# The chunked scan of an RWKV-7 layer: an even pace for its triangular solve, block-wise transfers, the group norm's weight and bias on GpSimd, key copies ahead of masks

## The chip, the cores and the metric

The kernel runs on one core of a Trainium2 chip. The metric is the device time of one execution in microseconds, the median over several. The core has TensorE (PE), VectorE (DVE), ScalarE (ACT), GpSimd (POOL) and SyncE (SP), whose queue issues most of the DMAs. Each engine takes its instructions in order and waits on semaphores that others set.

## The reference

A trunk of two layers with 1024 channels runs over two requests that share the weights: a prompt of 256 tokens and a sample of 1024. Layer 0 mixes tokens with a bidirectional RWKV-7 scan, layer 1 with neighbourhood attention, and each is followed by a squared-ReLU MLP. The change touches the scan and the group norm behind it. Cut to those, with 16 heads of 64 channels:

```
def step(S, inp):                       # in both directions, d = 0 and 1
    r_t, w_t, k_t, v_t, a_t, b_t = inp
    sa = einsum('bhvk,bhk->bhv', S, a_t)
    S = S * w_t + sa[..., None] * b_t + v_t[..., None] * k_t
    return S, einsum('bhvk,bhk->bhv', S, r_t)
y = scan forward + scan backward
mu, var = mean and variance of y over the 64 channels of a head
y = ((y - mu) * rsqrt(var + GN_EPS)) * lnx_g + lnx_b
y = y + bonus * v                       # bonus: one number per head and token
out = (y * g) @ w_o
```

## The kernel before

**Jobs and steps.** The scan works on chunks of 64 tokens. A job is sixteen chunks of a pair of heads (one head in each half of the 128 partitions): jobs 0 and 1 take four head pairs of the prompt each, four chunks long, and jobs 2 to 9 one head pair each of the sample. That is 10 jobs of 16 steps; in each step the forward direction does one chunk and the backward direction another. Within a step (`scan_step`) PE adds products of keys and values into the PSUM banks `bx` and `by`, ACT copies a part out as `up` (L1031), PE multiplies it by the chunk's inverse `Q`, ACT copies the result as `u` (L1051), PE adds its products, and ACT scales the next state `S` (L1066). The output goes to `y`: by an ACT copy in the first eight steps (L1072), by a DVE addition in the last eight (L1074). Each step also prepares the keys of a later step: PE makes `kps` (L952, a PSUM tile with one buffer), DVE multiplies it by a mask into `zz` (L957), and ACT copies the rest as `ll` (L962).

**The inverse.** Each chunk and direction needs the inverse of a triangular 64x64 matrix. In `scan_job`, for each of eight pieces of a job (direction d and group g of four chunks), a load `eab` (L813), products `aps` on PE (L821), a mask on DVE into `za` (L824) and a store to the DRAM scratch `dd` (L827) prepare it. `mload` (L842) loads the 32x32 diagonal blocks back, with one block in each partition, the second direction's as `mraw`, which GpSimd copies transposed into `mt` (`mtr`, L851, four copies). Then DVE solves all blocks at once: 31 steps, one rank-1 update each, a multiplication `tmp` (L867) and an addition to `q` (L869); the first and last steps are one instruction (L863). The result goes through DRAM (`qd`, L880 and L883) into the halves of the tiles `qq` and `qx` (L901, L902), and two products on PE with ACT copies in between (`yps`/`yt`, `qps`/`qq`, L913 to L930) merge the diagonal blocks to the full inverse.

**The norm.** `scan_post` follows each half of a job's output, at clocks 12.9 and 16.9 of the job, so that its last part lies in steps 1 and 5 of the next: bonus times v on DVE into `bv` (L1104), mean, centred `y` (L1112), squares on ACT into `ysq` (L1116), variance (L1120), a reciprocal root and the scaling of `y` (L1137). PE transposes `y` into `zps` and `bv` into `vps` (L1143). ACT scales `zps` by the norm's weight and adds the bias, which stand per partition after the transposition (L1149, four instructions), DVE adds `vps` (L1153), and eight DMAs store the tile `zt` into `z_d` (L1158).

**Order.** All this is written as closures with times, `at(t, f)`, in units of a step; a job's clock starts at 16 times its number. The list is sorted by time and emitted, and PE, DVE, ACT and GpSimd take the instructions in just that order; SP's queue is ordered by the framework. Items of job 0 with times up to `hi` run beside the projections before the scan. PSUM tiles with the tag `aps` (`aps`, `yps`, `qps`, `zps`, `vps`) share two buffers.

Of the kernel before, what the change touches and what calls it, by code (L numbers as in the profile page):

```python
# [29 lines left out]
V_QG, V_KG, V_LG, V_LB = 136, 137, 138, 154  # L30
NVEC = 170
# [18 lines left out]
class Trunk:  # L50
# [50 lines left out]
    def l0_proj(self):  # L101
# [361 lines left out]
        def begin():  # L463
            bctx.close()
            self.scan_begin()

            hi, c = -5.0, ((-41.0, tb), (-18.0, tb + 6.0), (-5.0, tb + 17.0))
            for x in self.todo:
                if x[3] < 3 and x[0] <= hi:
                    (x0, t0), (x1, t1) = c[:2] if x[0] < -18.0 else c[1:]  # L470
# [247 lines left out]
    def scan_begin(self):  # L718
# [9 lines left out]
                                        (("vv", [P, 16, 64]), ("qq", [P, 16, 2, 64]), ("qx", [P, 16, 2, 64])))  # L728
# [21 lines left out]
    def scan(self):  # L750
# [7 lines left out]
        grow(self.r_x, "qx", [P, 16, 2, 64])  # L758
        for r in (self.r_q, self.r_x):
            nc.gpsimd.memset(r[0][1], 0.0)  # L760
        grow(self.r_za, "za", [P, 4, 64], 12)
        self.r_x4 = [[], 0]
# [24 lines left out]
    def scan_job(self, j):  # L787
# [14 lines left out]
        T0 = -36.0  # L802

        def first():
            J["dd"] = [self.dsc.tile([16, 2, 64, 64], F32, name="dd", tag="dd") for _ in range(2)]
        at(T0 - 2.0, first, E)
        for n, (d, g) in enumerate(order):
# [18 lines left out]
            def store(d=d, g=g):  # L826
                nc.sync.dma_start(J["dd"][d].rearrange("c e s t -> (e s) c t")[:, 4 * g:4 * g + 4, :], J["za", d, g])  # L827
# [8 lines left out]
        def mload():  # L836
            mt = self.er.tile([P, 32, 32], F32, name="mt", tag="mt")
            raw = self.er.tile([P, 32, 32], F32, name="mraw", tag="mraw")
            for d in range(2):
                for b in range(2):  # L840
                    o, bs = 64 * d + 32 * b, slice(32 * b, 32 * b + 32)
                    nc.sync.dma_start((mt, raw)[d][o:o + 32], J["dd"][d].rearrange("c e s t -> (c e) s t")[:, bs, bs])  # L842
# [12 lines left out]
        T3, load = T2, 0.0  # L855
        for jj in range(31, 0, -1):
# [15 lines left out]
            if load > 930.0:  # L872
                T3, load = T3 + 0.5, 0.0
# [17 lines left out]
        at(T3 - 6.0, qclear)  # L891

        def qld():
            src = lambda x, o: J["qd"][x, o:o + 32].rearrange("(c e) s t -> e s c t", e=2)
            for d in range(2):
                for b in (d, 1 - d):
                    o, bs = 64 * d + 32 * b, slice(32 * b, 32 * b + 32)
                    for e in range(2):
                        q0 = slice(64 * e + 32 * b, 64 * e + 32 * b + 32)
                        if b == d:  # L900
                            nc.sync.dma_start(J["qx"][q0, :, d, bs], src(1 - d, o)[e])  # L901
                        nc.sync.dma_start(J["Q"][q0, :, d, bs], src(d, o)[e])  # L902
        at(T3 + 1.6, qld)

        for n, (d, g) in enumerate(order):
            m, c0 = grp[g]

            def merge1(c, d=d, g=g):
                if c == 0:
                    J["yps", d, g] = w4(self.pa.tile([P, 512], F32, name="yps", tag="aps"))  # L910
                for c in (c, c + 1):
                    for es, eo in HALVES:
                        mm(J["yps", d, g][es, c], J["za", d, g][es, c], J["qx"][es, 4 * g + c, d], start=True, stop=True)  # L913
# [13 lines left out]
            def merge2c(d=d, g=g):  # L927
                for e in range(2):
                    rl = slice(64 * e + 32 * d, 64 * e + 32 * d + 32)
                    nc.scalar.copy(J["Q"][rl, 4 * g:4 * g + 4, d, 32 - 32 * d:64 - 32 * d], J["qps", d, g][rl, :, :32])  # L930

            t = 2 * n - 5 if n > 1 else -3 + n
            for dt, f in ((0.12, lambda f=merge1: f(0)), (0.14, lambda f=merge1: f(2)), (0.5, merge1c), (0.76, lambda f=merge2: f(0)), (0.78, lambda f=merge2: f(2)), (0.97, merge2c)):
                at(t + dt, f)
# [7 lines left out]
        for q in range(16):  # L942
# [24 lines left out]
        def vload():  # L967
            J["v"] = self.nxt(self.r_v)
            vd = self.scr["v_d"]
            parts = [(grp[0][0], grp[0][1], 0, 16)] if grp[0][1] else [(m, c0, 4 * g, 4) for g, (m, c0) in enumerate(grp)]  # L970
            for m, c0, k, n in parts:
                rows = slice(c0 * L, (c0 + n) * L)
                for e, (es, eo) in enumerate(HALVES):
                    nc.sync.dma_start(J["v"][eo, k:k + n], vd[rows, m * P + 64 * e:m * P + 64 * e + 64].rearrange("(c s) v -> s c v", s=L))
        at(-5.423, vload)
# [110 lines left out]
    def scan_post(self, at, J, grp, left):  # L1086

        nc = self.nc
        for half in range(2):
# [15 lines left out]

            def p1(st=st, y=y):
# [32 lines left out]
            def tr(src, nm, st=st):  # L1139
                ps = st[nm] = self.pa.tile([P, 4, 2, 64], F32, name=nm, tag="aps")  # L1140
                swap = self.ident.rearrange("p (e t) -> p e t", e=2)[:, ::-1]
                for b in range(4):
                    nc.tensor.matmul(ps[:, b], src()[:, b // 2, b % 2 * 2:b % 2 * 2 + 2], swap, start=True, stop=True)  # L1143

            def trc(st=st, runs=runs):
                zt = st["zt"] = self.yp.tile([P, 4, 2, 64], F32, name="zt", tag="zt", bufs=1)
                for x, (m, c0) in enumerate(runs):
                    for e in range(2):
                        nc.scalar.activation(zt[:, 2 * x:2 * x + 2, e], st["zps"][:, 2 * x:2 * x + 2, e], AF.Identity, scale=self.v(V_LG, 2 * m + e), bias=self.v(V_LB, 2 * m + e))  # L1149
# [10 lines left out]
            if left == 0 and half == 1:  # L1160
                when = (-2.0, -0.1, 0.0, 0.1, 0.2, 0.3, 0.4, 0.5, 0.6, 0.7, 0.8, 0.9, 1.0)
            else:
                when = (0.2, 0.6, 0.95, 1.15, 1.45, 1.6, 1.75, 1.95, 2.3, 3.36, 4.36, 3.52, 4.6)
            bv = lambda st=st: st["bv"].rearrange("p (x c) v -> p x c v", x=2)
            for dt, f in zip(when, (p0, p1, p2, p2b, p2c, lambda f=p3: f(0), lambda f=p3: f(1), lambda f=p3: f(2), p4,
                                    lambda f=tr, y=y: f(y, "zps"), lambda f=tr, bv=bv: f(bv, "vps"), trc, p5)):
# [714 lines left out]
def host_layout(inputs):  # L1881
# [25 lines left out]
        np.tile(i["na_q_g"][0], 2)[:, None], np.tile(i["na_k_g"][0], 2)[:, None],  # L1907
        *(np.tile(i[nm].reshape(16, 64).T, (2, 1)) for nm in ("rw_lnx_g", "rw_lnx_b"))], 1)
# [36 lines left out]
```

## Time and profile before

| | us |
|---|---|
| median of 3 runs | 4202.09 (4198.46 to 4203.69) |
| the profiled execution, its own time | 4200.77 |
| its span, first to last instruction | 4199.0 |
| first and last `up` copy of the scan, from the span's start | 761.9 and 1444.4 |
| PE busy over the span | 3811.6 (91%) |
| DVE, ACT, GpSimd busy over the span | 2490.4, 1549.7, 1141.8 |

A row of a timeline reads: start, duration, engine, line, operation, output and inputs; in brackets the engine's idle time just before it and what ended it. A row of the waits reads: the waiting engine, tile and line, the one that released it, and then the time in total, the number of waits and the longest. A row of groups has the count, busy time and the mean of one in ns, and behind the bar the idle time before. A row of windows has the length of the stretch, the busy time of PE, of PE's weight loads, of DVE, ACT and GpSimd with their instruction counts, TensorE's granted clock, the busy share of the DMA engines and GB/s. The scan, 682.5 of the span's 4199.0 us by its first and last `up`, is the part to look at.

### The profile page before, as it was taken

To read this page: it belongs to the slowest core of one execution; us is meant where nothing else is said; L and a number is where in the kernel's file an instruction comes from. 1 tells how busy PE (TensorE), PEld (TensorE's weight loads), DVE (VectorE), ACT (ScalarE), POOL (GpSimd) and SP (SyncE) were. 2 spreads that over 40 slices of the span, in tenths; PEclk is the share of its full clock that TensorE was granted. 3 is DMA by queue.
4 is the path that set the end of the run, shared out by engine and by line. 5 is a ranking of instruction groups with operands and counts; after the bars stand their busy time and mean duration, and the time that the engine had idled before them with its cause. 6 is when DMAs were issued, how large, how long until landed. Compare 5 with 4: busy or idle time off the path is not lost.

```text
span 4199.0 us, 88054 instructions
## 1 busy us (share of the span) xinstructions
PE 3811.6 (91%) x35700; PEld 3197.4 (76%) x35700; DVE 2490.4 (59%) x4870; ACT 1549.7 (37%) x3711; POOL 1141.8 (27%) x1014
## 2 busy tenths in 40 slices
PE   7887879677777799999999999999989999999999
PEld 4664669666766688888888889776767788888888
DVE  7888973556666357555555561456565755555555
ACT  6776651344444442111111132455554211111111
POOL 5440001001010134222222250334344422222222
PEclk8996889899999899999999999999999999999999
DMA  3326565756564351111111115333333111111111
GB/s 110 88 95 205 197 192 148 181 147 164 144 166 119 87 166 46 41 41 41 38 37 38 41 56 165 90 80 74 81 101 128 61 41 36 36 41 41 36 36 61
DMA packets 443255, 387.81 MB, mean 92 GB/s; under 512 B 223296, under 2 KB 367904, under 8 KB 442848
## 3 DMA queue, kind: packets, MB, share of 16 engines
q1 hardware_dynamic: 394336, 314.92, 26.7%
q10 hardware_dynamic: 46704, 61.35, 4.3%
q8 instruction: 280, 4.59, 0.5%
q0 software_dynamic: 1808, 5.90, 0.4%
q14 instruction: 127, 1.04, 0.1%
HBM read 272.05 MB, written 121.24 MB: 94 GB/s over the span
## 4 chain that ended last, share of the span: by engine, by line
PE 58%; DVE 4%; ACT 3%; DMA 2%; issue 1%; POOL 1%; SPq 1%; ACTq 0%; DVEq 0%; POOLq 0%
PE ps L96 17%; PE ps L98 17%; PE ps L97 17%; PE pt L1802 1%; PE op L1860 1%; PE by L989 1%; PE nst L1597 1%; PE s L1784 1%; PE s L1787 1%; PE vps L512 1%; PE vps L513 1%; PE vps L514 1%; PE bx L989 1%; PE kps L952 0%; DMA vs_d<-v_d 0%
## 5 line engine op out<-in xcount | busy, mean ns | idle before, releaser
L1417 DVE TENSOR_TENSOR x<-ps,x 128x256 f32<-128x256 f32 x1488 | 814.7, 597 | 629.0 <-PE ps L98 628.6
L96 PE MATMUL ps<-ah,whi 128*128 128x512 f32 (+1 forms) x2304 | 843.5, 366 | 4.2 <-ACT whi L90 3.5
L98 PE MATMUL ps<-ah,wlo 128*128 128x512 f32 (+1 forms) x2304 | 824.3, 358 | 2.0 <-POOL wlo L91 2.0
L97 PE MATMUL ps<-al,whi 128*128 128x512 f32 (+1 forms) x2304 | 823.8, 358 | 0.0
L91 POOL TENSOR_TENSOR wlo<-raw,whi 128x1024 fp32r<-128x1024 f32 (+1 forms) x178 | 390.2, 2192 | 861.1 <-ACT whi L90 833.1
L96 PE MATMUL ps<-hh,whi 128*128 128x512 f32 (+1 forms) x1536 | 547.3, 356 | 13.0 <-DVE x L1417 13.0
L98 PE MATMUL ps<-hh,wlo 128*128 128x512 f32 (+1 forms) x1536 | 546.1, 356 | 0.0
L97 PE MATMUL ps<-hl,whi 128*128 128x512 f32 (+1 forms) x1536 | 545.6, 355 | 0.0
L96 PEld LDWEIGHTS ps<-ah,whi 128*128 128x128 f32 x2304 | 438.7, 190 | 78.7 <-issue 13.1
L98 PEld LDWEIGHTS ps<-ah,wlo 128*128 128x128 f32 x2304 | 437.6, 190 | 68.1 <-POOL wlo L91 2.9
L97 PEld LDWEIGHTS ps<-al,whi 128*128 128x128 f32 x2304 | 438.5, 190 | 60.2 <-issue 1.1
L90 ACT CAST whi<-raw 128x1024 fp32r<-128x1024 f32 (+1 forms) x206 | 200.8, 975 | 703.0 <-PE ps L97 627.9
L96 PEld LDWEIGHTS ps<-hh,whi 128*128 128x128 f32 x1536 | 291.8, 190 | 56.6 <-DVE x L1417 15.8
L98 PEld LDWEIGHTS ps<-hh,wlo 128*128 128x128 f32 x1536 | 291.7, 190 | 41.1
L97 PEld LDWEIGHTS ps<-hl,whi 128*128 128x128 f32 x1536 | 291.7, 190 | 41.1
L1396 POOL TENSOR_TENSOR rl<-rl 128x512 f32<-128x512 f32 (+1 forms) x192 | 174.1, 907 | 500.5 <-PE ps L98 458.3
L1395 ACT ACTIVATE rl<-ps 128x512 f32<-128x512 f32 (+1 forms) x192 | 100.8, 525 | 546.3 <-PE ps L98 546.3
L1398 ACT CAST hh<-rl 128x512 fp32r<-128x512 f32 (+1 forms) x192 | 105.5, 549 | 320.9 <-POOL rl L1396 320.9
L1399 DVE TENSOR_TENSOR hl<-rl,hh 128x512 fp32r<-128x512 f32 (+1 forms) x192 | 119.4, 622 | 151.5 <-ACT hh L1398 151.0
L989 PE MATMUL by<-up,qq 64*64 64x64 f32 x1280 | 75.6, 239 | 111.1 <-ACT up L1031 106.7
L1795 POOL TENSOR_TENSOR s<-s,mx 128x384 f32<-128x384 f32 (+1 forms) x154 | 116.9, 769 | 213.8 <-DVE mx L1794 144.9
L957 DVE TENSOR_TENSOR zz<-kps,cst 128x512 f32<-128x512 f32 x160 | 110.2, 688 | 79.9 <-PE kps L952 79.9
(308 smaller groups left out, 7685.9 us busy)
## 6 DMA issues: line engine op xcount, KB each, us to landing
x<-x_d SPq DMA_DIRECT2D x88, 512.0 KB, 4.6
raw<-in_w_down_dram SPq DMA_DIRECT2D x64, 512.0 KB, 3.2
raw<-in_w_up_dram SPq DMA_DIRECT2D x64, 512.0 KB, 3.1
eab<-x_d SPq DMA_DIRECT2D x80, 256.0 KB, 6.0
x_d<-ar ACTq DMA_DIRECT2D x32, 512.0 KB, 2.8
x_d<-bk ACTq DMA_DIRECT2D x32, 512.0 KB
bs<-tab SPq DMA_DIRECT2D x128, 96.0 KB, 3.8
v_d<-vt ACTq DMA_DIRECT2D x80, 128.0 KB, 4.3
```

Source lines behind the costliest of these rows:

```text
L90: nc.scalar.copy(hi[:, cs], raw)
L91: lo_eng.tensor_tensor(out=lo[:, cs], in0=raw, in1=hi[:, cs].bitcast(F32), op=ALU.subtract)
L96: mm(ps, sh, mh, start=first, stop=False)
L97: mm(ps, sh, ml, start=False, stop=False)
L98: mm(ps, sl, mh, start=False, stop=last)
L957: nc.vector.tensor_tensor(out=z, in0=src[:, :, :, :P], in1=self.mask[d].unsqueeze(1).unsqueeze(1).to_broadcast([P, 2, 2, P]), op=ALU.mult)
L989: mm = lambda out, a, b, start, stop: nc.tensor.matmul(out, a, b, start=start, stop=stop, skip_group_check=True)
L1396: nc.gpsimd.tensor_tensor(out=r[:, :n], in0=r[:, :n], in1=r[:, :n], op=ALU.mult)
L1398: nc.scalar.copy(hh[:, :n], r[:, :n])
L1399: nc.vector.tensor_tensor(out=hl[:, :n], in0=r[:, :n], in1=hh[:, :n].bitcast(F32), op=ALU.subtract)
L1417: nc.vector.tensor_tensor(out=xv, in0=ps[:, :n], in1=xv, op=ALU.add)
L1795: nc.gpsimd.tensor_tensor(out=s[:, :nk], in0=s[:, :nk], in1=mx[:, 2:3].to_broadcast([P, nk]), op=ALU.mult)
```

## The change

It has five parts.

- **The solve's pace.** The 31 rank-1 updates come 0.8 of a slot apart instead of 0.5 (a slot holds two of them), from step 9 of the job two ahead to step 5 of the job just ahead; before, they lay between step 14.5 and step 6. The preparation of each job (`T0`) starts earlier.
- **Whole blocks.** `dd` holds the diagonal blocks only, each contiguous, so that `mload` reads rows of 4 KB; a piece's store is four DMAs instead of one. `qx` has half its width, the loads of `qx` and `qq` come one pair at a time instead of in a burst, the merge's first product is 32 columns wide, its copies `yt` go into tiles that hold the constant part already, and its last copy is one instruction instead of two, half a step later.
- **The norm.** Weight and bias come as a tile `lnx`, with the values along the free axis. GpSimd adds the bias to `bv` and multiplies `y` by the weight. PE transposes both into the same PSUM tile, and one ACT copy makes `zt`. That tile now has the tag `ysq`, so it shares the one buffer of the squares.
- **Key copies.** `ll` is emitted ahead of `zz`.
- **Products.** The products `aps` stand between the step's last matmuls and the key products in odd steps, and v is loaded in two parts.

```diff
-            hi, c = -5.0, ((-41.0, tb), (-18.0, tb + 6.0), (-5.0, tb + 17.0))
+            hi, c = -6.0, ((-42.0, tb), (-19.0, tb + 6.0), (-6.0, tb + 17.0))
...
+        self.r_yt = [[[], 0], [[], 0]]
...
-        T0 = -36.0
+        T0 = (-37.0, -37.0, -39.0)[j] if j < 3 else -41.5
...
-            J["dd"] = [self.dsc.tile([16, 2, 64, 64], F32, name="dd", tag="dd") for _ in range(2)]
+            J["dd"] = [self.dsc.tile([2, 16, 2, 32, 32], F32, name="dd", tag="dd") for _ in range(2)]
...
             def store(d=d, g=g):
-                nc.sync.dma_start(J["dd"][d].rearrange("c e s t -> (e s) c t")[:, 4 * g:4 * g + 4, :], J["za", d, g])
+                for e in range(2):
+                    for b in range(2):
+                        o, bs = 64 * e + 32 * b, slice(32 * b, 32 * b + 32)
+                        nc.sync.dma_start(J["dd"][d][b, 4 * g:4 * g + 4, e].rearrange("c s t -> s c t"), J["za", d, g][o:o + 32, :, bs])
...
-            for d in range(2):
-                for b in range(2):
-                    o, bs = 64 * d + 32 * b, slice(32 * b, 32 * b + 32)
-                    nc.sync.dma_start((mt, raw)[d][o:o + 32], J["dd"][d].rearrange("c e s t -> (c e) s t")[:, bs, bs])
...
+            for d in (1, 0):
+                for b in range(2):
+                    o = 64 * d + 32 * b
+                    nc.sync.dma_start((mt, raw)[d][o:o + 32], J["dd"][d][b].rearrange("c e s t -> (c e) s t"))
...
-        T3, load = T2, 0.0
+        T3, load, pace = T2, 0.0, (-11.0 - T2) / 15
...
             if load > 930.0:
-                T3, load = T3 + 0.5, 0.0
+                T3, load = T3 + pace, 0.0
...
-        at(T3 + 1.6, qld)
+        for i in range(8):
+            d, b, e = i // 2 % 2, i // 4 ^ i // 2 % 2, i % 2
+            at(T3 + 1.5 + 0.3 * i, lambda x=(d, b, e): qld(*x))
...
             def merge1c(d=d, g=g):
-                yt = J["yt", d, g] = self.rp.tile([P, 4, 64], F32, name="yt", tag="yt", bufs=3)
-                nc.scalar.copy(yt, J["yps", d, g])
+                yt = J["yt", d, g] = self.nxt(self.r_yt[d])
+                nc.scalar.copy(yt[:, :, 32 * d:32 * d + 32], J["yps", d, g][:, :, :32])
...
-            for dt, f in ((0.7, lambda f=kprod: f(0)), (0.72, lambda f=kprod: f(1)), (0.95, kmask), (1.02, kcopy)):
+            for dt, f in ((0.7, lambda f=kprod: f(0)), (0.72, lambda f=kprod: f(1)), (0.95, kmask), (0.74, kcopy)):
...
+            def lnx(k, st=st, runs=runs, y=y):
+                t = (y(), st["bv"].rearrange("p (x c) v -> p x c v", x=2))[k]
+                for x in range(1 if runs[0][0] == runs[1][0] else 2):
+                    sl = slice(0, 2) if runs[0][0] == runs[1][0] else slice(x, x + 1)
+                    w = self.lnx[:, k, runs[x][0]].unsqueeze(1).unsqueeze(1).to_broadcast([P, sl.stop - sl.start, 4, 64])
+                    nc.gpsimd.tensor_tensor(out=t[:, sl], in0=t[:, sl], in1=w, op=(ALU.mult, ALU.add)[k])
...
-            def tr(src, nm, st=st):
-                ps = st[nm] = self.pa.tile([P, 4, 2, 64], F32, name=nm, tag="aps")
...
                 for b in range(4):
-                    nc.tensor.matmul(ps[:, b], src()[:, b // 2, b % 2 * 2:b % 2 * 2 + 2], swap, start=True, stop=True)
...
+                    for k, src in enumerate((y(), bv)):
+                        nc.tensor.matmul(ps[:, b], src[:, b // 2, b % 2 * 2:b % 2 * 2 + 2], swap, start=k == 0, stop=k == 1)
...
             def p5(st=st, runs=runs):
-                zt = st["zt"]
-                nc.vector.tensor_tensor(out=zt, in0=st["vps"], in1=zt, op=ALU.add)
+                zt = self.yp.tile([P, 4, 2, 64], F32, name="zt", tag="ysq", bufs=1)
+                nc.scalar.copy(zt, st["zps"])
```

What this makes of the order on three engines:

ACT, step 1 of a middle job, before; `yt` and `qq` are the merge's copies, `ysq` the squares of the norm's second half:

```order
L1051 COPY u<-by_7425 128x128 [waits PE_49,Activation_49]
L917 COPY yt<-yps 128x256
L1066 ACTIVATE S<-bx_7423,dall 128x64 [waits PE_49]
L1066 ACTIVATE S<-bx_7423,dall 128x64
L1072 COPY y<-by_7425 128x2x64 [waits PE_49]
L930 COPY qq_7373<-qps 32x4x32 [waits PE_49]
L930 COPY qq_7373<-qps 32x4x32
L962 COPY ll<-kps 128x256 [waits DVE_49]
L1116 ACTIVATE ysq<-y 128x512
L1031 COPY up<-bx_7422 128x128 [waits PE_49,Activation_49]
```

The same place now:

```order
L1063 COPY u<-by_7467 128x128 [waits DVE_49,PE_49]
L925 COPY yt_7424<-yps 128x4x32
L1168 COPY zt<-zps 128x512
L1078 ACTIVATE S<-bx_7465,dall 128x64 [waits PE_49]
L1078 ACTIVATE S<-bx_7465,dall 128x64
L973 COPY ll<-kps 128x256 [waits PE_49]
L1084 COPY y<-by_7467 128x2x64
L1135 ACTIVATE ysq<-y 128x512 [waits DMAHW3_49,DMAHW4_49,DMAHW2_49,DMAHW5_49,DMAHW1_49,DMAHW6_49,DMAHW0_49,DMAHW7_49,DVE_49,Activation_49]
L1043 COPY up<-bx_7464 128x128 [waits PE_49]
```

`ll` waits for PE instead of DVE and stands ahead of the `y` copy, the copy `zt` has come in, and `ysq` waits for eight DMA semaphores.

SP, the load of a solve's blocks, before:

```order
L827 DMA dd<-za_7386 128x4x64 [waits DMAHW1_49,DVE_49]
L939 DMA x_7392<-x_d 128x4x256 [waits DMAHW2_49,PE_49]
L813 DMA eab_6422<-x_d 128x2x256 [waits DMAHW3_49,PE_49]
L842 DMA mt<-dd 32x32x32 [waits DMAHW7_49,DMAHW4_49]
L842 DMA mt<-dd 32x32x32 [waits DMAHW5_49]
L842 DMA mraw<-dd 32x32x32 [waits DMAHW6_49,DMAHW1_49]
L842 DMA mraw<-dd 32x32x32
```

And now, behind the last of eight stores `z_d`:

```order
L1173 DMA z_d<-zt 64x2x64 [waits DMAHW3_49]
L841 DMA dd<-za_7410 32x4x32 [waits DMAHW4_49,DVE_49]
L841 DMA dd<-za_7410 32x4x32 [waits DMAHW5_49]
L841 DMA dd<-za_7410 32x4x32 [waits DMAHW6_49]
L841 DMA dd<-za_7410 32x4x32 [waits DMAHW7_49]
L912 DMA qx_7398<-qd 32x16x32 [waits DMAHW0_49]
L913 DMA qq_7397<-qd 32x16x32 [waits DMAHW1_49]
L912 DMA qx_7398<-qd 32x16x32 [waits DMAHW2_49]
L913 DMA qq_7397<-qd 32x16x32 [waits DMAHW3_49]
L860 DMA mraw<-dd 32x1024 [waits DMAHW6_49,DMAHW4_49]
L860 DMA mraw<-dd 32x1024 [waits DMAHW7_49,DMAHW5_49]
```

The load has moved from the end of a job to a place behind the norm's stores and among the loads of the previous solve's result; `mraw` goes first, and `mt` follows it.

DVE, one step with the solve beside it, between two masks, before:

```order
L957 TENSOR_TENSOR zz<-kps,cst 128x512 [waits PE_49]
L867 TENSOR_TENSOR tmp<-mt,q 128x207 [waits DVE_49]
L869 TENSOR_TENSOR q<-q,tmp 128x9x23 [waits DVE_49]
L867 TENSOR_TENSOR tmp<-mt,q 128x192 [waits DVE_49]
L869 TENSOR_TENSOR q<-q,tmp 128x8x24 [waits DVE_49]
L867 TENSOR_TENSOR tmp<-mt,q 128x175 [waits DVE_49]
L869 TENSOR_TENSOR q<-q,tmp 128x7x25 [waits DVE_49]
L867 TENSOR_TENSOR tmp<-mt,q 128x156 [waits DVE_49]
L869 TENSOR_TENSOR q<-q,tmp 128x6x26 [waits DVE_49]
L957 TENSOR_TENSOR zz<-kps,cst 128x512 [waits PE_49]
```

And now, in a step of a job's second half:

```order
L968 TENSOR_TENSOR zz<-kps,cst 128x512 [waits Activation_49]
L881 TENSOR_TENSOR tmp<-mt,q 128x135 [waits DVE_49]
L883 TENSOR_TENSOR q<-q,tmp 128x27x5 [waits DVE_49]
L881 TENSOR_TENSOR tmp<-mt,q 128x156 [waits DVE_49]
L883 TENSOR_TENSOR q<-q,tmp 128x26x6 [waits DVE_49]
L1086 TENSOR_TENSOR y<-by_7466,y 128x2x64 [waits PE_49,Activation_49]
L968 TENSOR_TENSOR zz<-kps,cst 128x512 [waits Activation_49]
```

Two pairs stand between two masks instead of four, and the mask waits for ACT's key copy.

More of the change, by code (lines that the diff above doesn't have):

```diff
@@ L29 @@
 V_GMIX, V_GMLP, V_MIX, V_W0, V_A0, V_KK, V_KA, V_RK = 0, 16, 32, 80, 96, 112, 120, 128
[L30 to L31 removed]
+V_QG, V_KG = 136, 137
+NVEC = 138
 C_ID, C_MF, C_MB, C_ONE, C_SEL = 0, 128, 256, 384, 386
@@ L761, in scan @@
         grow(self.r_za, "za", [P, 4, 64], 12)
+        self.lnx = rp.tile([P, 2, 8, 64], F32, name="lnx")
+        nc.sync.dma_start(self.lnx.rearrange("p a m v -> p (a m v)"), self.a["lnx"])
+        self.r_yt = [[[], 0], [[], 0]]
+        for d in range(2):
+            grow(self.r_yt[d], f"yt{d}", [P, 4, 64], 2)
+            for t in self.r_yt[d][0]:
+                nc.gpsimd.memset(t, 0.0)
+                for e in range(2):
+                    hi = slice(32 - 32 * d, 64 - 32 * d)
+                    rows = slice(64 * e + hi.start, 64 * e + hi.stop)
+                    nc.gpsimd.tensor_copy(t[rows, :, hi], self.ident[rows, rows].unsqueeze(1).to_broadcast([32, 4, 32]))
         self.r_x4 = [[], 0]
@@ L927, in merge2c @@
             def merge2c(d=d, g=g):
[L928 to L933, printed above, removed]
+                nc.scalar.copy(J["Q"][:, 4 * g:4 * g + 4, d, 32 - 32 * d:64 - 32 * d], J["qps", d, g][:, :, :32])
+            t = 2 * n - 5
+            for dt, f in ((0.12, lambda f=merge1: f(0)), (0.14, lambda f=merge1: f(2)), (0.5, merge1c), (0.76, lambda f=merge2: f(0)), (0.78, lambda f=merge2: f(2)), (1.5, merge2c)):
                 at(t + dt, f)
```

62 lines of the change are left out of this document (29 added, 33 removed).

## Prediction

> **What bounds the kernel now.** I read the page's chain that ended last first, then the windows for the scan alone, and then the waits of ACT and PE in the scan, since the change touches nothing else. The profiled execution is 4200.8 us (span 4199.0), 1.3 us under the median of 4202.1; the sum below is made against 4200.8, and 1.3 is inside what a measurement of this kernel can tell from no change, 0.2% or 8.4 us.
>
> ```profile
> PE 58%; DVE 4%; ACT 3%; DMA 2%; issue 1%; POOL 1%; SPq 1%; ACTq 0%; DVEq 0%; POOLq 0%
> 762.00:1444.00 682.00, 526.21 (x16952) 470.79 (x16952) 409.35 (x1031) 321.29 (x1211) 69.62 (x101) 0.94 0.57 144
> L1031 ACT COPY up<-bx x160: 248/271/273, 761.9 to 1444.4; 128x128 f32<-128x128 f32 x160
> PE by L989 <- ACT up L1031: 106.7, 106, 3.3
> PE bx L989 <- issue: 9.9, 8, 3.1
> ACT u L1051 <- PE by L989: 144.8, 159, 4.8
> ACT ll L962 <- DVE zz L957: 87.2, 89, 2.9
> ACT S L1066 <- PE by L989: 60.4, 107, 4.1
> ```
>
> Over the whole kernel PE carries the chain; in the scan (761.9 to 1444.4, one `up` copy in each of 160 steps) it does not. There PE works 526 of 682 us, DVE 409, ACT 321, GpSimd 70: nobody is full. PE's largest idleness is behind ACT's `up`, and `up` sits on ACT behind the key copy `ll`, which waits 87.2 us in 89 waits for DVE's mask `zz`. So a step is a ring of dependences PE, ACT, PE, ACT, with a detour over DVE at its end.
>
> Time per job is read from the first `up` of job 1 and of job 8:
>
> ```profile
> 823.85 0.27 ACT L1031 COPY up<-bx 128x128 f32<-128x128 f32 x1
> 1323.32 0.27 ACT L1031 COPY up<-bx 128x128 f32<-128x128 f32 x1
> ```
>
> 499.47 us over seven jobs is 71.4 us a job, or 4.46 a step. A clean step, in ACT's timeline and PE's and DVE's beside it:
>
> ```profile
> 944.71 0.27 ACT L1031 COPY up<-bx 128x128 f32<-128x128 f32 x1
> 945.59 0.27 ACT L1051 COPY u<-by 128x128 f32<-128x128 f32 x1 [0.60 <-PE by L989]
> 946.42 0.52 ACT L1066 ACTIVATE S<-bx,dall 128x64 f32<-128x64 f32 x2 [0.56 <-PE by L989]
> 946.19 0.83 PE L952 MATMUL kps<-x 64*64 64x192 f32 x16
> 947.09 0.69 DVE L957 TENSOR_TENSOR zz<-kps,cst 128x512 f32<-128x512 f32 x1 [0.27 <-PE kps L952]
> 947.82 0.37 ACT L962 COPY ll<-kps 128x256 f32<-128x256 f32 x1 [0.88 <-DVE zz L957]
> 948.16 0.27 ACT L1031 COPY up<-bx 128x128 f32<-128x128 f32 x1
> ```
>
> It takes 3.45 us, and its last 0.88 is ACT waiting for `zz`.
>
> **Key copies ahead of masks.** Now `ll` waits for PE's kps alone and `zz` for `ll`. kps ends at 947.02; with `ll` right there it starts about 0.1 later, and `up` 0.3 after it, instead of 947.82 and 948.16: 0.75 off a step. `zz` starts 0.3 later, but its results are wanted steps later, and what stands behind it on DVE is not on the ring in these steps. In odd steps the products (half of 16 matmuls per piece) and the second merge stand on PE's path; I leave them near the 3.6 to 3.7 that they have, with 0.4 a job as gain. Even steps 8, 10 and 12 give 0.75 each; in 4 and 6 the `y` copy stands in the way too, so I take 0.47. That is 3.2 + 0.4 = 3.6 a job.
>
> **Pacing.** The solve's rank-1 pairs come two to a step over 14 steps instead of four over seven or eight. Where they were dense, `zz` queued behind them. Job 6, steps 2 and 3:
>
> ```profile
> 1194.96 0.26 ACT L1031 COPY up<-bx 128x128 f32<-128x128 f32 x1
> 1199.37 0.37 ACT L962 COPY ll<-kps 128x256 f32<-128x256 f32 x1 [1.76 <-DVE zz L957]
> 1204.15 0.37 ACT L962 COPY ll<-kps 128x256 f32<-128x256 f32 x1 [1.26 <-DVE zz L957]
> 1204.42 0.27 ACT L1031 COPY up<-bx 128x128 f32<-128x128 f32 x1
> ```
>
> Two steps take 9.46 us. By the ring without that wait an even one is 2.9 and an odd one 3.66, 6.56 together: 2.9 a job gained, from pacing and key copies alike. Steps 13 to 0, where the norm's DVE operations meet the solve, I leave unchanged: less solve there at once, but the same sum of DVE work and two GpSimd operations more.
>
> **Norm's weight and bias, one transposition, one buffer.** Per half job, four ACT scalings and DVE's addition go, and one ACT copy (128x512, 0.63 by `ysq`'s row below) writes `zt`. PE does as many transposing matmuls, now all eight together. But `zt` now takes the buffer of the squares, `ysq`. In step 1 ACT does `zt`, S, `ll`, `y`, `ysq`, `up` in that order, and `ysq` waits for all eight stores of `zt` to land. Queued behind it is `up`, and PE waits for that. Job 6's step 1 before:
>
> ```profile
> 1185.37 0.27 ACT L1031 COPY up<-bx 128x128 f32<-128x128 f32 x1
> 1187.51 2.07 PE L1143 MATMUL vps<-cst,bv 128*128 128x128 f32 x8 [1.33 <-DVE za L824]
> 1190.31 0.27 ACT L1051 COPY u<-by 128x128 f32<-128x128 f32 x1 [4.67 <-PE by L989]
> 1194.42 0.63 ACT L1116 ACTIVATE ysq<-y 128x512 f32<-128x512 f32 x1
> 1190.40 6.02 SPq L1158 DMA_DIRECT2D z_d<-zt  x8
> L1158 SPq DMA_DIRECT2D z_d<-zt x160: 574/597/1650, 831.7 to 1469.2; - x160
> DMA to landing us min/median/max: 1.9/2.0/3.5
> ```
>
> After: the wait of 1.33 for `za` goes, so the eight matmuls end 2.2 after `up`, `u` comes at 2.5, `zt` ends at 3.5. Eight stores at 0.6 to 0.75 each put the last issue at about 8.6, its landing 2.0 later at 10.6, `ysq` 0.5, `up` at 11.1. Before, 1185.37 to 1194.96 was 9.6: 1.5 a job lost. Without the shared buffer the step would be near 6.3, so this one wait eats about 4.8 a job. Step 5 has the transposition too, but no `ysq` behind it: nothing, 5.7 before against 5.6.
>
> The GpSimd operations (four of 128x512 a job) sit beside DVE operations. How that went elsewhere in this kernel:
>
> ```profile
> L1137 DVE TENSOR_TENSOR y<-y,rqr 128x512 f32<-128x512 f32 x19 | 13.0, 684 | 0.0
> L1382 DVE TENSOR_TENSOR x<-x,ms 128x512 f32<-128x512 f32 x16 | 24.3, 1565 | 0.1
> L1396 POOL TENSOR_TENSOR rl<-rl 128x512 f32<-128x512 f32 x128 | 133.6, 1044 | 498.5 <-PE ps L98 458.3 <-ACT rl L1395 40.2
> ```
>
> An operation of DVE with two SBUF inputs takes 0.68 in the scan and 1.57 beside GpSimd's half of the same line, 0.88 more. Two of the four fall into steps 13 to 0, where DVE is dense: 1.8 a job if nothing covers it. DVE is idle 40% of the scan, so I take nothing and keep 1.8 a job (14 in all) for the range.
>
> The Trainium skill, page "SBUF — State Buffer", section "SBUF: two separate sides", says that DVE and GpSimd share a port pair that one holds exclusively, so that the later one stands for the other's whole instruction. The row agrees in kind. By the rule each uncovered operation would cost up to its whole 1.04, 2.1 a job instead of 1.8, and the sum would still not show it while DVE has slack.
>
> **Whole blocks: the load of the solve.** SP's queue gets four stores of `dd` for one, 24 more a job, and the block load `mraw` comes behind eight `z_d` stores, four `dd` stores and four loads of `qx`/`qq`. The rows:
>
> ```profile
> dd<-za SPq DMA_DIRECT2D x80, 128.0 KB, 3.2
> 909.16 0.59 SPq L827 DMA_DIRECT2D dd<-za  x1
> 1236.33 4.27 SPq L842 DMA_DIRECT2D mraw<-dd  x2
> DMA to landing us min/median/max: 3.4/3.4/3.4
> 1242.88 2.41 POOL L851 COPY mt<-mraw 64x256 f32<-64x256 f32 x4 [21.63 <-DMA mraw<-dd]
> 1246.88 0.28 DVE L863 SCALAR_TENSOR_TENSOR q<-mt,q 128x31 f32<-128x31 f32 x1
> ```
>
> Before, GpSimd's copies ended at 1245.3 and DVE came to the first rank-1 at 1246.9, 1.6 in hand. After, counted from step 5's `up`: `z_d` stores issued by 9.3, four `dd` stores at 0.5 by 11.3, four q loads at about a store's 0.59 by 13.6, `mraw` waits for the stores to land until about 14, lands at 17.4, copies until 19.8. DVE reaches the first rank-1 at step 9, about 15.3 (5.6 + 2.9 + 3.7 + 2.9). It stands 4.3 to 4.5 us, and behind it stand `zz` and the `y` additions; kps has one buffer, so PE's next key products wait too. Of this I take half, 2.2 a job; the bounds are 0 (the chain is 4.5 shorter) and 5.
>
> The merge's narrower products, whole copies and spread q loads take a copy of 0.26 off ACT per piece and a burst off SP; they lie beside the ring and I price them at nothing; uncovered, the 0.26 would be another 2 a job of gain at most.
>
> **Ramp.** The solve of the first jobs runs before the scan, beside the projections, and starts one step earlier, with 24 more stores on a queue on which PE already waits:
>
> ```profile
> 738.41 1.12 PE L821 MATMUL aps<-eab 64*64 64x64 f32 x16 [6.71 <-DMA eab<-x_d]
> ```
>
> 24 stores at 0.59 would be 14 if all were exposed. I take 6, with 0 and 12 as bounds.
>
> **Sum.** A middle job: 3.6 + 2.9 − 1.5 − 2.2 = 2.8 gained, times seven (jobs 1 to 7) 19.6. Job 8 has no load of a solve behind it: 5.0. Job 0 has no norm in its first steps but few steps with a dense solve: 3.6. Job 9: 1 lost in step 1. Ramp: 6 lost. Together 21: 4180.
>
> **The rivals.**
> *The gain without its losses* (4130; 4100 to 4160): the load comes in time (15), the ramp costs nothing (6), and the stalls of PE on issue go, since the products stand elsewhere (9.9 by its row). 21 + 30 is 51 off, and near 4100 if step 1's stores land sooner. For it: every term is a queue length that I added up, not one that a row shows. Against: DVE's 1.6 in hand and the 4.27 that `mraw` takes already.
> *Slower: DVE blocked at the first rank-1* (4222; 4206 to 4245). The place is step 9 of each job, and the mechanism the load above, with DVE standing before `tmp`/`q` and so `zz`, kps and PE behind it. It turns the sum when it costs 3 us more a job than the 2.2 taken; 6 more (8.2, if a queue of SP ahead of `mraw` waits for a landing once more, 3.2 to 3.4 each) is 42 lost in seven jobs against 21 gained. For it: a wait of DVE on the load is in the trace before too.
>
> ```profile
> DVE q L863 <- POOL mt L851: 4.1, 2, 3.5
> ```
>
> Against: DVE's idle 40%, and that only two such waits stand in the scan, 3.5 the longer.
> *The change does not do what it says* (4200): step 1's `ysq` wait and DVE's total leave the ring where it was, and `ll` ahead of `zz` only moves the wait onto the mask; 4192 to 4209.
>
> **How the numbers follow.** The forecast, 4180 (4160 to 4192), has 0.40; the gain without losses 0.24; slower 0.26; nothing left 0.10, of it 0.08 within 0.2%. Faster by over 0.2% (below 4193.7) is 0.40 + 0.24 less a little for its upper edge, 0.63; within 0.2% 0.08; slower (above 4210.5) 0.29. The range of 8 in 10 takes in most of both rivals: 4108 to 4228.
>
> **What would show it.** Right: `ll` waits for PE and no longer for `zz`; even steps of 2.6 to 2.9; in step 1, ACT's `ysq` waits some 4 to 5 us for a DMA of `zt`; DVE's first rank-1 waits for GpSimd's `mt` by 2 to 6 us in each job. Wrong, towards faster: that last wait missing. Wrong, towards slower: zz or `tmp` waiting over 8 us in a job, a first `up` later than 768, or even steps that stay at 3.4.

## The result and the profile after

The changed kernel takes 4244.1 us (median of 4 runs, 4242.2 to 4244.9) against 4200.3 us of the kernel before in the same job: a ratio of 1.0103, interval 1.0085 to 1.0120. It is 44 us slower, where 20 us faster was forecast. The profiled execution is 4244.8 us, its span 4243.1.

The first `up` of the scan, from ACT's timeline:

```profile
768.70 0.27 ACT L1043 COPY up<-bx 128x128 f32<-128x128 f32 x1
```

It came 6.8 us later than before (761.9), and the scan, from that `up` to its last (1492.7), takes 724.0 us instead of 682.5. What lies behind the scan is 4.2 us shorter. So the 44 us are 6.8 + 41.5 − 4.2. The 41.5 can be placed by adding up the time from `up` to `up`, step by step, over all ten jobs of both traces:

| steps of a job | after less before, all jobs | a middle job (mean of jobs 2 to 7), before | after |
|---|---|---|---|
| 1 | +27.7 | 9.35 | 11.80 |
| 2, 3 | −14.4 | 9.52 | 7.81 |
| 4 to 9 | −14.7 | 23.95 | 22.72 |
| 10 to 12 | +48.6 | 10.13 | 16.10 |
| 13 to 0 | −5.7 | 18.47 | 17.97 |

Two places lose 76 us, the rest gains 35. The waits of three engines, from 740 to 1500 us, name both places. DVE first:

```profile
DVE zz L968 <- ACT ll L973: 112.6, 104, 4.6
DVE q L877 <- POOL mt L865: 27.6, 4, 7.9
DVE q L877 <- DMA mt<-dd: 12.3, 2, 6.2
DVE q L877 <- DMA x<-x_d: 11.6, 1, 11.6
DVE q L877 <- DMA qx<-qd: 6.2, 1, 6.2
DVE q L877 <- DMA dd<-za: 5.3, 1, 5.3
```

The waits of `q` are one each at the first rank-1 of a solve. Eight of them, 58 us together, lie in the scan, where there were 4.1 us in two before; the ninth, with `dd` as releaser, ends at 760.7, ahead of the first `up`. The releasers differ because only the last of several is named; that what they wait for is the load of the blocks and its copies is shown by the runs that move the load. ACT and PE:

```profile
ACT ll L973 <- PE kps L963: 120.9, 153, 7.5
ACT ysq L1135 <- DMA z_d<-zt: 34.4, 6, 6.1
ACT ysq L1135 <- DVE y L1131: 28.6, 11, 4.2
ACT ysq L1135 <- DMA dd<-za: 19.4, 3, 6.6
```

```profile
PE by L1001 <- ACT up L1043: 113.9, 86, 7.3
PE by L1001 <- DVE y L1086: 30.2, 11, 5.1
```

The key copy waits for PE now and no longer for the mask, as the change says. `ysq` waits 54 us in nine jobs for DMAs. PE waits 30 us for DVE's `y` addition, a wait that was not there before.

**Step 1**, job 4, ACT's timeline with SP's below:

```profile
1073.43 0.28 ACT L1043 COPY up<-bx 128x128 f32<-128x128 f32 x1
...
1076.34 0.60 ACT L1168 COPY zt<-zps 128x512 f32<-128x512 f32 x1
...
1085.05 0.63 ACT L1135 ACTIVATE ysq<-y 128x512 f32<-128x512 f32 x1 [6.54 <-DMA dd<-za]
1085.59 0.25 ACT L1043 COPY up<-bx 128x128 f32<-128x128 f32 x1
```

```profile
1077.18 6.18 SPq L1173 DMA_DIRECT2D z_d<-zt  x8
```

`zt` is done 3.5 us after `up`, the last of eight stores is issued at 1083.4, and `ysq` starts 1.7 after that, with the next `up` behind it: 12.2 us. The row names a store of `dd` as the releaser, as in three of the nine waits; in the other six it is `z_d`. That the eight stores of `zt` are what counts is shown below by the run that gives `zt` another buffer.

**Steps 9 to 11**, job 4 again. SP, GpSimd and DVE, and then ACT and PE:

```profile
1100.05 5.35 SPq L1173 DMA_DIRECT2D z_d<-zt  x8
1105.50 2.52 SPq L841 DMA_DIRECT2D dd<-za  x4
1108.06 0.44 SPq L912 DMA_DIRECT2D qx<-qd  x1
...
1110.66 0.49 SPq L913 DMA_DIRECT2D qq<-qd  x1
1111.25 0.90 SPq L860 DMA_DIRECT2D mraw<-dd  x2
```

```profile
1115.79 2.04 POOL L865 COPY mt<-mraw 64x256 f32<-64x256 f32 x4 [13.76 <-DMA mraw<-dd]
```

```profile
1110.97 0.69 DVE L968 TENSOR_TENSOR zz<-kps,cst 128x512 f32<-128x512 f32 x1 [0.68 <-ACT ll L973]
1117.86 0.27 DVE L877 SCALAR_TENSOR_TENSOR q<-mt,q 128x31 f32<-128x31 f32 x1 [6.20 <-POOL mt L865]
...
1118.56 0.28 DVE L1086 TENSOR_TENSOR y<-by,y 128x128 f32<-128x128 f32 x1
```

```profile
1114.50 0.27 ACT L1043 COPY up<-bx 128x128 f32<-128x128 f32 x1 [0.38 <-PE bx L1001]
...
1119.73 0.52 ACT L1078 ACTIVATE S<-bx,dall 128x64 f32<-128x64 f32 x2 [3.98 <-PE by L1001]
```

```profile
1118.90 0.27 PE L1001 MATMUL by<-vv,zz 64*64 64x64 f32 x1 [3.34 <-DVE y L1086]
```

The queue of SP runs without a gap from the stores of `zt` to `mraw`. DVE is free at 1111.66 and stands 6.2 us for the copies of `mt`. Behind it stands the `y` addition that empties a bank of `by`. PE's next matmuls into `by` wait 3.3 us for that addition, ACT's `S` comes 4 us late, and the next `up` is at 1123.0: a step of 8.5 us.

TensorE's granted clock (the third number from the end of a row of windows) changed there too. The end of step 10 and then step 11, and below them step 11 of the same job before:

```profile
1118.90:1123.00 4.10, 2.89 (x72) 2.41 (x74) 3.26 (x12) 0.89 (x4) 0.00 (x0) 0.56 0.39 59
1123.00:1127.77 4.77, 4.65 (x134) 4.47 (x131) 2.98 (x8) 1.59 (x6) 0.00 (x0) 0.66 0.95 282
```

```profile
1087.42:1090.79 3.37, 2.30 (x88) 2.00 (x88) 1.16 (x3) 1.32 (x6) 0.00 (x0) 1.00 0.67 114
```

Behind the wait the clock was 0.56 and then 0.66, and PE was busy for 4.65 of the 4.77 us of step 11, with 134 matmuls instead of 88. How much of step 11 is the clock's and how much the work's no run separates: with the first rank-1 later (below), so that it falls into step 11, the clock stays at 1.00 in steps 10 to 12 of the middle jobs and step 11 still takes 4.5.

### The profile page after: what moved, and what is told of

Its sections match the earlier page's. It is cut to its first block, busy times and chain, and to the rows that moved or that the text cites. A ratio compares the mean times of both kernels' runs of the same rounds, so it can differ in the third digit from the quotient of the medians.

```text
span 4243.1 us, 88135 instructions
## 1 busy us (share of the span) xinstructions
PE 3830.2 (90%) x35700; PEld 3227.4 (76%) x35700; DVE 2491.5 (59%) x4850; ACT 1503.7 (35%) x3571; POOL 1198.5 (28%) x1074
## 4 chain that ended last, share of the span: by engine, by line
PE 69%; DVE 14%; ACT 5%; DMA 4%; issue 3%; SPq 3%; POOL 2%; ACTq 0%; DVEq 0%; POOLq 0%
PE ps L96 17%; PE ps L97 17%; PE ps L98 17%; PE kps L963 2%; PE by L1001 2%; PE bx L1001 2%; SPq L1173 1%; PE vps L512 1%; PE vps L513 1%; PE vps L514 1%; PE zps L1164 1%; PE op L1874 1%; PE pt L1816 1%; DVE q L883 1%; DVE tmp L881 1%
## 5 line engine op out<-in xcount | busy, mean ns | idle before, releaser
L96 PE MATMUL ps<-hh,whi 128*128 128x512 f32 (+1 forms) x1536 | 547.7, 357 | 11.6 <-DVE x L1431 11.6
L96 PEld LDWEIGHTS ps<-ah,whi 128*128 128x128 f32 x2304 | 439.8, 191 | 77.5 <-issue 11.8
L963 PE MATMUL kps<-x 64*64 64x192 f32 x2560 | 175.6, 370 | 20.5 <-DVE zz L968 15.6
```

Of the source, the lines that this page charges most:

```text
L96: mm(ps, sh, mh, start=first, stop=False)
L963: mm(J["kp"][out, e, 192 * c:192 * c + 192], x[es, b, 2 * pr + c], x[es, 2:5, 2 * pr + c], start=True, stop=True)
```

## The experiments

All ratios are against the kernel before, run in the same job. "A middle job" is the mean of jobs 2 to 7 in the profiled execution.

### zt in another buffer

```diff
-                zt = self.yp.tile([P, 4, 2, 64], F32, name="zt", tag="ysq", bufs=1)
+                zt = self.yp.tile([P, 4, 2, 64], F32, name="zt", tag="bv", bufs=2)
```

> The changed kernel, but the tile zt takes a buffer of bv (free since the transposition) instead of the one of the squares, so that the squares of the norm's second half no longer wait for eight stores to land. Theory (the shared buffer costs about 5 us a job in step 1): step 1 falls from 11.8 us to 6.5 to 7, nine jobs gain about 45 us, 4200 us (4190 to 4212). Rival (DVE is behind in that stretch anyway, so that its centred y comes late and takes the wait's place): half or less of it, 4222 us or more. Steps 10 and 11 stay at 8.7 and 4.6 us by both.

4190.9 us, ratio 0.9977 (0.9966 to 0.9987): 53 us less than the changed kernel, from one tag. (The profiled execution is the fastest of ten, 4181.1; 8 us of what it is shorter by lie behind the scan, where the edit changes nothing.) A middle job's step 1 is 7.0 instead of 11.8, and over all jobs step 1 goes from 27.7 above to 15.9 below the kernel before. ACT's timeline of job 6's step 1 shows what is left of the wait:

```profile
1194.75 0.28 ACT L1043 COPY up<-bx 128x128 f32<-128x128 f32 x1
1197.65 0.61 ACT L1168 COPY zt<-zps 128x512 f32<-128x512 f32 x1
...
1201.25 0.63 ACT L1135 ACTIVATE ysq<-y 128x512 f32<-128x512 f32 x1 [1.43 <-DVE y L1131]
1201.79 0.25 ACT L1043 COPY up<-bx 128x128 f32<-128x128 f32 x1
```

`ysq` now waits 1.4 us for DVE, and not for a DMA in any job. Taking the shared buffer away gives back more than the change had lost, and by the traces 44 us of it lie in step 1.

### The first rank-1 later, and both

```diff
-        T2 = T1 + 1.9
+        T2 = T1 + 4.3
```

> The changed kernel, with the first rank-1 update 2.4 steps later (step 11.4 instead of 9) and the pace so much denser (0.64 of a step instead of 0.8) that the solve ends where it did; all transfers are where they were. Theory (DVE stands at the first rank-1 until the load's transposed copies are there, and the y additions, the masks and PE stand behind it: 6 to 7 us a job): steps 10 and 11 fall from 8.7 and 4.6 to about 3 each, 4190 us (4180 to 4208). Rival (the solve's work on DVE is what costs, and it only moves into steps 12 to 5): 4230 us or more. Step 1 stays near 11.8 by both.

4226.3 us, ratio 1.0065 (1.0053 to 1.0077): between theory and rival. The wait at the first rank-1 went (4.9 us in three, from 58 in eight) and a middle job's steps 10 and 11 fell from 13.1 to 7.9 us; but step 0 rose from 3.4 to 6.9 and step 1 from 11.8 to 13.2. The same edit on top of the other buffer:

> Both edits of the two runs before it in the changed kernel. Theory (two separate waits, on ACT in step 1 and on DVE in step 10): the gains add up, 4148 us (4135 to 4165). Rival (what the one gives is taken by the other, since both only let DVE catch up): not under 4180 us.

4176.1 us, ratio 0.9945 (0.9932 to 0.9957): outside the theory's range, nearer to the rival, 15 us under the run with the other buffer alone. In its windows, job 5's steps 13 to 0 are

```profile
1161.94:1181.11 19.17, 13.03 (x403) 11.62 (x400) 18.41 (x45) 6.57 (x27) 4.38 (x3) 0.89 0.76 222
```

19.2 us, of which DVE works 18.4 (the third pair of numbers). The denser solve has little room there: against the run with the other buffer, a middle job's steps 10 to 12 gain 4.4 us and the other steps lose 2.7, so starting late moves more than half of the loss.

### Key copies alone, in the kernel before

```diff
-(0.95, kmask), (1.02, kcopy))
+(0.95, kmask), (0.74, kcopy))
```

> The kernel before with one edit, the key copy ll emitted ahead of the mask zz (0.74 instead of 1.02). Theory (the ring of a step runs over zz): even steps fall from 3.4 to 2.6 to 2.9, steps 2 and 3 by 1 to 2 us together, 3.6 to 5 us a job, 4162 us (4150 to 4172). Rival (the wait moves to PE's next key products, which need zz to have read the one buffer of kps): within 8 us of the kernel before.

4197.3 us, ratio 0.9996 (0.9987 to 1.0005): the rival's time, though not by the rival's wait, which is 1.4 us in all. Steps 10 to 12 do fall (3.4 each to 2.7, 3.0 and 3.1) and so do 2 and 3 (9.5 to 6.9 together), 40 us over all jobs. But step 1 rises from 9.35 to 10.1, 4 from 3.55 to 4.8 and 5 from 5.7 to 7.7: what the ring gives early is owed to DVE, which has a solve to finish by step 6. The place where PE pays is the norm's transpositions in steps 1, 4 and 5, which wait for DVE's mask `za`. The waits before, and with the key copies ahead:

```profile
PE vps L1143 <- DVE za L824: 14.3, 14, 1.6
```

```profile
PE vps L1143 <- DVE za L824: 31.2, 14, 3.2
PE zps L1143 <- DVE za L824: 6.6, 8, 1.1
PE kps L952 <- DVE zz L957: 1.4, 3, 0.7
```

The windows of steps 2 to 5 of one job, before and with the key copies ahead:

```profile
1194.96:1213.67 18.71, 14.35 (x464) 12.68 (x464) 15.89 (x44) 9.20 (x37) 0.30 (x1) 1.00 0.51 131
```

```profile
1120.48:1139.78 19.30, 14.18 (x464) 12.64 (x464) 16.38 (x46) 9.31 (x36) 0.00 (x0) 1.00 0.51 129
```

DVE (the third pair of numbers) works 15.9 of 18.7 us, and 16.4 of 19.3, at the same granted clock.

### The same with half of the solve

```diff
+                if jj % 2 == 0:
+                    return
```

> The kernel of e4_keys (before, with key copies ahead of masks) with every second rank-1 update of the solve left out of the computation, at unchanged times. Theory (key copies ahead gave nothing in sum since DVE is full from step 13 to step 5, with the dense solve, and what even steps gain is lost there): steps 13 to 5, 49 us in e4_keys, fall by 8 to 12 us a job, 4110 us (4095 to 4130). Rival (those steps wait for PE, its clock and transfers, not for DVE): 4180 us or more.

The kernel leaves out every second rank-1 update. 4136.1 us, ratio 0.9856 (0.9839 to 0.9874), 61 us under the run with the whole solve; the theory was right for steps 1 to 5, not for steps 13 to 0, and expected more. Steps 1 and 2 to 5 of one job:

```profile
1144.13:1151.17 7.04, 4.52 (x140) 4.08 (x136) 5.68 (x13) 3.01 (x10) 0.00 (x0) 1.00 0.42 99
1151.17:1167.08 15.91, 13.89 (x464) 12.59 (x464) 10.83 (x30) 9.31 (x37) 0.00 (x0) 1.00 0.62 156
```

In a middle job step 1 fell from 10.1 to 7.0 and steps 2 to 5 from 19.4 to 16.0. Steps 13 to 0 stayed (19.6 and 19.3), so there it is not DVE that binds the kernel before with this edit. In steps 1 to 5 it is.

### Where the load stands in SP's queue

The loads of `qx` and `qq` 0.7 of a step later, so that `mraw` goes ahead of four of them (on the kernel with `zt` in another buffer):

> The kernel of e1_zt_in_bv (zt in a buffer of bv), with the loads of qx and qq 0.7 of a step later, so that SP's queue takes mraw and mt ahead of the four q loads that stood between the last dd store and mraw. Theory (the first rank-1 is late by SP's queue, 3.0 us of which are these four loads): DVE's wait for mt and steps 10 and 11 (7.6 and 4.6 us) fall by about 3 us together, eight jobs, 4168 us (4158 to 4180). Rival (mraw waits for the dd stores to land in any case, so nothing of the queue counts): steps 10 and 11 stay above 11 us together, 4185 us or more.

4179.0 us, ratio 0.9946 (0.9933 to 0.9958), 12 us less where 23 were expected: steps 10 and 11 fell from 12.2 to 11.6 in a middle job, above 11 as by the rival, and the rest came in job 1. In a middle job the four loads are thus only a small part of what makes the first rank-1 late.

The preparation of jobs 3 to 9 1.7 steps earlier, the solve where it was:

```diff
-        T0 = (-37.0, -37.0, -39.0)[j] if j < 3 else -41.5
+        T0 = (-37.0, -37.0, -39.0)[j] if j < 3 else -43.2
...
+        T2 = T1 + 1.9 if j < 3 else -23.0
```

> The kernel of e1_zt_in_bv, with the preparation of jobs 3 to 9 (products, masks, dd stores and the load mraw and mt) 1.7 steps earlier, so that the load stands ahead of the norm's eight z_d stores on SP; the rank-1 updates stay at step 9 with the pace of 0.8. Theory (a queue of SP, not the solve's work, is what DVE stands for in step 10): the wait of DVE for mt goes in the seven jobs, steps 10 and 11 fall from 12.1 to about 6, steps 13 to 1 stay within 1 us, 4152 us (4140 to 4166). Rival (DVE's work from step 9 to 5 is the bound, as the late rank-1 runs suggest, and the time comes back in steps 12 to 1): 4175 us or more.

4177.4 us, ratio 0.9939 (0.9926 to 0.9953); the total is the rival's, but not for its reason. DVE's waits for the load, all that are left, and PE's for the loads that now stand behind:

```profile
DVE q L878 <- DMA dd<-za: 11.4, 1, 11.4
```

```profile
PE qps L939 <- DMA qq<-qd: 6.5, 4, 2.2
```

A middle job's step 10 is 2.9 us instead of 7.6, and steps 13 to 1 did not grow beyond 0.5: DVE had room for the solve. Part of the loss came back at step 11 (5.6, where the merge needs `qq`, now queued behind `z_d`) and in job 0, whose load I had left where it was: one step of 13.6 us. SP's queue had only been reordered.

### The blocks as before

One store of `dd` per piece and strided loads again, in the kernel of the last run:

```diff
-                for e in range(2):
-                    for b in range(2):
-                        o, bs = 64 * e + 32 * b, slice(32 * b, 32 * b + 32)
-                        nc.sync.dma_start(J["dd"][d][b, 4 * g:4 * g + 4, e].rearrange("c s t -> s c t"), J["za", d, g][o:o + 32, :, bs])
+                nc.sync.dma_start(J["dd"][d].rearrange("c e s t -> (e s) c t")[:, 4 * g:4 * g + 4, :], J["za", d, g])
```

> The kernel of e6_load_ahead with the blocks as before the change: one dd store per piece instead of four, and the load mraw and mt in strided rows. Theory (SP's queue is the bound behind step 10: 24 stores of 0.48 us fewer a job; in e6_load_ahead the q loads, now behind the z_d stores, are late for the merge in step 11): step 11 falls from 5.6 to about 3.5, and job 0's 13.6 us step falls, 4155 us (4145 to 4166). Rival (the strided load's small packets cost more than the stores save): 4177 us or more.

4158.1 us, ratio 0.9908 (0.9893 to 0.9923), 19 us less. Step 11 is 4.3 instead of 5.6, job 0 63.6 us instead of 71.6, and the first `up` comes at 761.0 instead of 768.9. The same edit in the changed kernel itself:

> The changed kernel with the blocks as before the change: one dd store per piece instead of four, and strided loads. Theory (the chain of the load gets 2.0 us shorter at the dd stores, and the strided load is as long as the contiguous one, 3.4 us): steps 10 and 11 fall by 1.5 to 2, 4228 us (4218 to 4238). Rival (whole blocks are what keeps the late load from costing more, as the pace alone in the kernel before suggests with its wait of 10 us): steps 10 and 11 grow, 4255 us or more.

4226.1 us, ratio 1.0065 (1.0053 to 1.0078), 18 us less than the changed kernel, as the theory had it, but at other places: 7.5 us in the ramp (first `up` at 761.2) and 10 in job 0's steps 10 to 12. A middle job's steps 10 and 11 stayed (13.4 against 13.1). The queue is shorter there, but the strided load lands later:

```profile
DMA to landing us min/median/max: 3.2/4.6/5.0
```

That is the tile `mraw` in this run; with whole blocks the median is 3.5. So the whole blocks do not make steps 10 and 11 shorter.

Job 2's preparation 2 steps earlier on top of the first of these two:

> The kernel of e9_one_store with job 2's preparation 2 steps earlier, its rank-1 updates where they were. Theory (the one long step left in job 0 is the load of job 2's solve): job 0 loses some 8 us, 8 us less than e9_one_store. Rival (the preparation then delays the first steps, whose queue is full already): the first steps of job 0 grow by as much, the same as e9_one_store.

4148.1 us, ratio 0.9880 (0.9867 to 0.9894), 10 us less. Of the 9.8 us between the two profiled executions, 8.3 lie behind the scan, where the edit changes nothing: job 0 lost 2.9 us where 8 were expected, the whole scan 3.7, and the first `up` came 2.2 later. Whether the edit itself is worth 10 us is therefore not shown. One short wait at a first rank-1 is left in the scan:

```profile
DVE q L875 <- POOL mt L864: 1.7, 1, 1.7
```

This is the fastest full version found: the change with `zt` elsewhere, one store per piece, and the load ahead of the norm's stores. It is 1.2% faster than the kernel before.

### The pace alone

The kernel before with the changed `T0`, `pace` and `hi` and nothing else. Its `qclear` then comes while the job that holds the tile has a step left, so that step's product uses a cleared inverse.

> The kernel before with the pacing alone (starts T0, pace and the bound of job 0's items), and all transfers, buffers and the order of masks and key copies as before. Theory (the pace puts the load behind eight z_d stores, one dd store and all twelve q loads, 2 us more than in the changed kernel): step 1 stays near 9.3, DVE waits for mt 7 to 9 us in each job in step 9 or 10, steps 2 and 3 gain 2 to 3, 4240 us (4222 to 4258). Rival (an even pace is a gain by itself, and the late load came with the block-wise stores): 4190 us or less.

4282.8 us, ratio 1.0194 (1.0180 to 1.0208), further than expected.

```profile
DVE q L863 <- POOL mt L851: 81.8, 8, 12.8
```

Seven jobs wait 10 to 13 us each, job 0 2.4: a middle job's step 9 is 14.1 us. Steps 2 and 3 gain 1.3 together, step 1 2.3. So the even pace brought the late load. SP's queue in job 4 shows what the changed kernel softened: here all twelve loads of `qx` and `qq`, from 1113.4 to 1121.8, go ahead of the blocks, there four of them in 3.1 us. The spread loads are the likely cause, though no run has them alone; the whole blocks are not, since steps 10 and 11 of the changed kernel are as long without them.

### GpSimd's four operations

The load-ahead kernel without norm's weight and bias.

> The kernel of e6_load_ahead without the four operations of GpSimd per job: norm's weight and bias are left out of the computation. Theory (each of them holds a DVE operation for 0.9 us, and DVE is what steps 13 to 1 wait for): 1.8 to 2.8 us a job less than e6_load_ahead, 16 to 28 us in all. Rival (DVE has slack there, and the four are hidden): within 8 us of e6_load_ahead.

4167.7 us, ratio 0.9917 (0.9903 to 0.9931): 10 us less, between theory and rival. A middle job's steps 13 to 1 fall by 2.0 us, as the theory had it, but its steps 10 to 12 grow by 1.2, and with the rest 1.1 a job are left. In the changed kernel, DVE and GpSimd at one such place:

```profile
1091.02 1.26 DVE L883 TENSOR_TENSOR q<-q,tmp 128x135 f32<-128x135 f32 x1
```

```profile
1090.86 1.27 POOL L1123 TENSOR_TENSOR y<-y,lnx 128x512 f32<-128x512 f32 x1 [13.05 <-DVE y L1156]
```

## Why the prediction was wrong, point by point

The term that turned the sign is the load of the solve, forecast at 2.2 us a job; it is the fourth point.

- **Key copies**, 3.6 a job: the ring does run over `zz`, and in the changed kernel even steps 4, 6, 8 and 12 fell to 2.8 to 3.2, near the 2.6 to 2.9 computed: 2.3 us of the 2.4 counted for them. What step 10 was to give is lost in the load. What the term leaves out is DVE. In the kernel before, key copies alone gave 40 us in steps 2, 3 and 10 to 12 and lost it again in 1, 4, 5 and around, where DVE must finish a solve; with half of the solve left out, step 1 and steps 2 to 5 fell by 6.4 us a job.
- **Pacing** (a slot of two updates every 0.8 of a step instead of every 0.5), 2.9 a job in steps 2 and 3: measured 1.7. Step 2 took 4.0 instead of 2.9. With `zt` in another buffer the gain is 2.5, so most of what is missing goes with the wait of step 1. I priced the pace by the wait that it removes and not by the load that it leaves no room for: the solve of one job ends at step 5 and the next begins at step 9, and between them all transfers of both stand on SP. The pace alone costs 82 us.
- **Step 1**, 1.5 lost: 2.5 measured, 11.8 against the 11.1 computed. The mechanism, `ysq` behind eight stores, is shown by the run that moves `zt`. It was seen as a small loss because I set it against the step before; against the step without that buffer it is 4.8 us a job, as the prediction says and then leaves.
- **The load of the solve**, 2.2 lost a job: this is the term that turned the sign. Its chain was nearly right: from step 5's `up` in job 4, first rank-1 reached at 15.4 us (15.3 forecast), stores out by 9.1 (9.3), `dd` by 11.7 (11.3), q loads by 14.9 (13.6), copies done at 21.5 (19.8), a wait of 6.2 (4.3 to 4.5). The step that failed is "of this I take half". In jobs 0 to 7 steps 10 to 12 grew by 6.5 us on average, while they shrank by 1.8 in job 8, which has no such load: 8.3 us a job, more than the wait itself. That figure also holds the solve's rank-1 updates, which job 8 has not, and the lower clock behind the wait, and the parts were not separated. The rival named this mechanism, with 8.2; that the figures are so near is luck, since its reason, one more landing that SP waits for, does not show: SP's queue ran without a gap. Moving the load away (without moving the solve) brought step 10 back to 2.9 and step 11 to 5.6, and gave 13.5 us in all against the run with `zt` in another buffer; with one store per piece it was 33. So no single run gives back the whole 8.3 a job.
- **GpSimd**, nothing taken, 1.8 a job kept: 2.0 in steps 13 to 1 of a middle job, 1.1 over the whole of it. The Trainium skill's rule (page "SBUF — State Buffer", section "SBUF: two separate sides") that the later of the two stands for the other's whole instruction agrees with the trace: `q`'s addition of 0.3 us took 1.26, started 0.16 after GpSimd's and ended 0.15 after it.
- **Ramp**, 6 lost: 6.8 measured; one store for the four takes 7.5 back.
- **Put at nothing**: step 5 took 0.9 more in the mean, by two jobs (7.1 and 9.8 us), in which PE was busy for 7.0 and 7.3 us at granted clocks of 0.76 and 0.83. Steps 13 to 0, left unchanged in the sum, fell by 0.5.
- **The rivals' sizes**: 42 us lost against 21 gained was 4222; the measured 4244 lies at the upper edge of that rival's range and above 4228, where the forecast's range of 8 in 10 ended. The faster rival's own 51 us would be 4150, not the 4130 set down for it.

What stays open: why steps 13 to 0 did not fall with half of the solve; how much of steps 10 to 12 is the granted clock's; and what the key copies are worth in the changed kernel, where taking out them alone was not run.

## What to carry to other kernels

An engine's idle share says nothing about a wait in an engine that takes its work in order: price such a wait by everything queued behind it, and ask which of that a ring of dependences needs. Before spreading a piece of work evenly, look at what must happen between its end and its next beginning, and which queue does it. And when a tile is given another tile's buffer, find the next writer of that buffer: if a DMA reads the tile, as `zt`'s stores do here, the writer waits for the landing, and everything behind it on its engine waits too.

## What the runs showed of the hardware

- The issue of a small DMA takes SP's queue 0.43 us (median) for a `dd` store and 0.60 for a `z_d` store: in the scan of the changed kernel, eight `z_d` stores in a row took 5.1 to 6.9 us and four `dd` stores 1.7 to 3.4. The 24 stores more a job, together with the contiguous load that they make possible, cost 18 and 19 us in two kernels.
- A load of 32x32 blocks in strided rows landed in 4.6 us (median) where the contiguous one took 3.5, and in 3.2 against 2.6 in the two kernels with the load ahead; in the kernel before, where it ran at the end of a job, the strided one took 3.4.
- TensorE's granted clock differed between equal stretches of one execution, here steps 2 to 5 of two jobs of the kernel before, the second of which is quoted above:

```profile
1122.90:1141.70 18.80, 16.25 (x464) 15.03 (x464) 15.96 (x44) 9.32 (x37) 0.30 (x1) 0.84 0.51 132
```

PE's 464 matmuls were busy for 16.25 us at 0.84 and for 14.35 at 1.00, and the stretch took 18.8 and 18.7 us: the clock did not set the length of these steps, in which DVE was busy for 16. In step 11 of the changed kernel, with PE busy nearly throughout, that can't be said.
